# Pinned places for squares, scalings and weight sums, and later places for two parts of the first group's output norm, in a two-scheme gemm kernel

## The chip, the cores and the metric

The kernel runs on one core of one Trainium2 chip. The metric is the device time of one execution in microseconds (us); the median over the runs shown counts. TensorE (PE) does the matrix products, VectorE (DVE), ScalarE (ACT) and GpSimd (POOL) do the elementwise work, and SyncE (SP) and POOL hand transfers to the DMA queues.

## The reference, cut to what matters

One layer over 2048 prompt tokens and 8 sequences of 8 new tokens, all in fp32, at width 2048:

```python
z = rms_norm(x, pre_g)
xr, gr, u, v, gs = split(z @ w_in)            # five blocks of 1024 columns
xc, new_buf = causal_depthwise_conv(xr, conv_buf, conv_w, conv_b)
hr, h_last = rg_lru(xc, ...)                  # two gates per head, then a scan over the tokens
br = hr * silu(gr)
u = gelu(u); v = rms_norm(gelu(v), sgu_g)
bs = chunk_spatial_gating(u, v, w_s, b_s) * silu(gs)
out = concat([br, bs]) @ w_out
y = x + rms_norm(out, post_g)
```

The results are y for the prompt and for the samples, the convolution and scan states, and the samples' normed v.

## The kernel before, in words

**Precision.** Each fp32 product runs as three passes in fp32r: high times high, high times low, low times high. So each weight piece (128x1024) is loaded by SP into `wraw` (L179), its high part `wh` is made by ACT (L187) and its low part `wl` by DVE (L195), and PE waits for both.

**Group 0.** The tokens are cut into four groups of 512; the first also holds the 64 sample tokens, 576 columns in all. Its stage is a plain gemm (L370, and L381 for v) over jobs of two pieces each (some 6.4 us of PE a piece): the `xr` and `gr` jobs first, then `v`, then `gs` and `u`, then the 16 `out` jobs. After a pair of heads, `lru0` runs the recurrence: exp, tanh, square and square root on ACT, products and two scans on DVE (L484 to L505), one product on POOL (L485). The order of instructions on each engine in this stage is not the order in which the program hands them in: the tile scheduler sorts them by priority and by the readiness that its cost model expects. `later`, which is `tc.keep_in_program_order` (L95), pins an instruction behind the instruction of the same engine that was handed in just before it. That sets its place in the queue and nothing else; the data it waits for are as before.

**Sums for the other groups.** Groups 1 to 3 use a scheme with seven products in place of eight, which needs sums of weight quadrants. They are made beside group 0's gemm for 28 units: 16 units `c` (pairs of column blocks of the input weight; their sums run on DVE), four `w_v` and eight `w_or` (sums on POOL). A unit is four 512 KB quadrant loads (`load_quadrants`, L237, handed to POOL's DMA queue), four chained adds (`make_sums`, L248, L250, L252, L254) and four stores of the sums (L245, POOL's queue), named P_c, P_w_v and P_w_or. The program hands in unit n's loads at 45+20.5n us and its sums at 64+20.5n us of a plain estimate of PE's time (L1133 to L1137). The four quadrants lie in slots of a ring of 13 large buffers (`dbl`); slots are given out in the order in which the program hands the work in.

**Group 1's input.** During group 0's out jobs the squares of group 1's x are summed (`stat_load` L620, `stat_sum` L628, on ACT), the inverse roots are spread over the partitions (L637, L646), and the x rows are loaded and scaled (`z_raw`, `z_norm` L656, on DVE).

**Groups 1 to 3.** This part is a manual schedule: steps of one weight piece each, with lists of work that go ahead of a step's products (`tasks`) and behind them (`late`), issued in the order written. The loop hands in a step's `hi` work, its tasks, its `lo` work, its products and then its late list (L1332 to L1342).

**Group 0's output.** `norm_a "o"` and `norm_b "o"` (`row_rstd`, `row_bcast`) turn the sum of squares of group 0's output into a scale for each token: two products with a matrix of ones (nsAo, nsBo), DVE work, and two more products (nsCo, nsDo) whose input `dgo` DVE makes (L294, L300). They are on the late lists of steps 4 and 10 of group 1. `finish0_*` then does for each of 16 blocks: a load (L602), a DVE scaling (L606), an add of x by DMA (L609) and a store (L612). Blocks 0 to 7 begin at steps 12, 14, ... 26, and blocks 8 to 15 at V+3, V+5, ..., where V is step 56, the first of group 1's v products.

Of the kernel before, what the change touches and what calls it, by code (L numbers as in the profile page):

```python
# [11 lines left out]
AF = mybir.ActivationFunctionType  # L12
ALU = mybir.AluOpType
# [11 lines left out]
TP = 512  # L25
# [15 lines left out]
C_PRE, C_POST, C_CW, C_CB, C_BR, C_BI, C_LAM, C_SG = 0, 16, 32, 64, 72, 80, 88, 96  # L41
# [13 lines left out]
def hybrid_layer(ctx: ExitStack, tc: tile.TileContext, a):  # L55
    nc = tc.nc
# [35 lines left out]
    def col(base, i):  # L92
        return cv[:, base + i:base + i + 1]

    later = tc.keep_in_program_order  # L95
# [48 lines left out]
    state = {}  # L144
# [94 lines left out]
    def make_sums(unit):  # L239
        nm = "_".join(str(x) for x in unit)  # L240
        t = state.pop(("quad", unit))

        def put(k, x):
            sums[unit, k] = hp.tile([P, W], F32, name=f"{k}_{nm}")
            side.dma_start(sums[unit, k], x)  # L245

        eng = nc.vector if unit[0] == "c" else nc.gpsimd
        eng.tensor_add(t["B11"], t["B11"], t["B12"])  # L248
        put("P1", t["B11"])
        eng.tensor_add(t["B12"], t["B12"], t["B22"])  # L250
        put("P3", t["B12"])
        eng.tensor_add(t["B22"], t["B22"], t["B11"])  # L252
        put("P2", t["B22"])
        eng.tensor_add(t["B21"], t["B21"], t["B22"])  # L254
        put("P4", t["B21"])
# [367 lines left out]
    def stat_sum(g, n):  # L623
        c, b = divmod(n, 2)
        if n == 0:
            state["xss", g] = mp.tile([P, 4, 2], F32, tag="xss", name=f"xss{g}")
        x = state.pop(("xs", g, n))
        nc.scalar.activation(x, x, AF.Square, accum_out=state["xss", g][:, c, b:b + 1])  # L628

    def stat_rstd(g):  # L630
        sv = mp.tile([P, 4], F32, tag="xsv", name=f"xsv{g}")
# [21 lines left out]
    def z_norm(g, j, rows=(0, 1)):  # L653
        x = state["R", g, j]
        for i in rows:
            nc.vector.scalar_tensor_tensor(x[:, i, :TP], x[:, i, :TP], col(C_PRE, 2 * j + i), state["rB", g],  # L656
                                           op0=ALU.mult, op1=ALU.mult)

    def parts(key, j):
        lo, hi = state[(*key, j)], state.get((*key, 4 + j))  # L660
# [84 lines left out]
    early, tasks, late = defaultdict(list), defaultdict(list), defaultdict(list)  # L745

    def at2(s, f, *args):

        tasks[s].append((f, *args))
# [309 lines left out]
    for job in jobs:  # L1059
        kind, j = job  # L1060
# [9 lines left out]
    for s in steps:  # L1070
        for job, i in s:
            kind, j = job
# [41 lines left out]
    for hp_ in range(0, NH, 2):  # L1114
        i = jobs.index(("gr", NH + hp_ + 1))
# [18 lines left out]
    for n, u in enumerate(units):  # L1134
        for t, f in ((45 + 20.5 * n, load_quadrants), (64 + 20.5 * n, make_sums)):
            by_step[next(i for i, x in enumerate(when) if x >= t)].append((f, u))
    for n in range(8):  # L1137
        at(("out", 3 + n // 2), stat_load, 1, n)
        at(("out", 5 + n // 2), stat_sum, 1, n)
# [3 lines left out]
    for j in range(8):  # L1143
        at(("out", 8 + j // 2), z_raw, 1, j)
        at(("out", 11 + j // 3), z_norm, 1, j)
# [17 lines left out]
    for n, step in enumerate(steps):  # L1163
        for f, *args in by_step[n]:
            f(*args)
        job, i = step[0]
# [37 lines left out]
    for g in range(1, NG):  # L1204
        G = len(steps2)
        V, U, O, R2 = G + 56, G + 84, G + 140, G + 168
# [22 lines left out]
        wide(g, "v", "w_v", 0, put_v(g))  # L1229
        if g == 1:  # L1230
            for j in range(KT):
                t = 12 + 2 * j if j < 8 else V + 3 + 2 * (j - 8)
                at2(t, finish0_load, j)
                t += 3
                at2(t, finish0_scale, j)
                at2(t + 1, finish0_add, j)
                at2(t + 4, finish0_store, j)
        else:
            at2(G - 1, load_gq, g - 1, 1)
            for n in range(4):  # L1240
                k = (g - 1, (1, 1, 0, 0)[n], (3, 2, 2, 3)[n])
                t = G + (5, 7, 9, 11)[n]
                at2(t, finish_scale, *k)
                at2(t + 1, finish_add, *k)
                at2(t + 6, finish_store, *k)
            at2(V + 16, load_gq, g - 1, 0)
            for n in range(4):
                k = (g - 1, n % 2, n // 2)
                t = V + 21 + 3 * n
                at2(t - 5, finish_load, *k)  # L1250
                at2(t, finish_scale, *k)
                at2(t + 1, finish_add, *k)
                at2(t + 6, finish_store, *k)
# [31 lines left out]
        if g + 1 < NG:  # L1285
            for n in range(8):
                at2(O + 2 + 3 * n // 2, stat_load, g + 1, n)
                at2(O + 5 + 3 * n // 2, stat_sum, g + 1, n)
            at2(O + 17, stat_rstd, g + 1)
            late[O + 20].append((stat_spread, g + 1))  # L1290
            at2(O + 21, stat_take, g + 1)
            for j in range(8):
                at2(O + 18 + j, z_raw, g + 1, j)
                for i in range(2):
                    at2(O + 22 + 2 * j + i, z_norm, g + 1, j, (i,))
            key = ("R", g + 1)
            for j in range(4):
                combine(key, "A11", j, R2 + 2 + j)
                combine(key, "A22", j, R2 + 8 + j)
                at2(R2 + 10 + j, pre, key, "D3", j)  # L1300
                combine(key, "A12", j, R2 + 12 + j)
                at2(R2 + 14 + j, pre, key, "E", j)
                combine(key, "E", j, R2 + 16 + j)
                at2(R2 + 18 + j, pre, key, "D1", j)
                combine(key, "D1", j, R2 + 19 + j)
                combine(key, "D3", j, R2 + 23 + j)
                at2(R2 + 21 + j, pre, key, "F", j)
                combine(key, "F", j, R2 + 26 + j)
# [15 lines left out]
    at2(R2 + 28, last_rstd, 0)  # L1324
    for qq in range(4):
        at2(R2 + 29, last_both, 0, qq)
    late[4].append((norm_a, "o"))
    late[10].append((norm_b, "o"))

    base = pos_of[steps2[0][3]]  # L1330
    with tc.manual_schedule():
# [84 lines left out]
```

## Time and profile before

| | us |
|---|---|
| median of 3 runs (lowest, highest) | 2570.75 (2570.57, 2571.52) |
| profiled execution, own time | 2568.9 |
| profiled execution, span | 2567.1 |
| PE busy | 2497.7 (97% of the span) |
| DVE busy | 1748.8 (68%) |
| ACT busy | 1391.6 (54%) |
| POOL busy | 470.5 (18%) |
| mean granted TensorE clock | 0.991 of full speed |

The span goes from the first to the last instruction; 1.8 us of the execution's own time lie around it. Group 0 takes the first 797 us of the span, groups 1 to 3 the rest. A row of the timeline gives the start, the duration, the engine, the line, what is written from what, and in brackets how long the engine stood idle before it and what ended that. Busy shares are means over stages with different limits, so the rows below are cut by stage.

### The profile page before, as it was taken

How to read it: one execution, taken by the hardware profiler on the slowest of the kernel's cores; microseconds unless marked ns; L12 is line 12 of the kernel's file. 1: busy time of each engine (PE TensorE's matmuls, PEld its weight loads, DVE VectorE, ACT ScalarE, POOL GpSimd, SP SyncE). 2: the span in 40 equal slices, each digit the busy share in tenths (PEclk: the TensorE clock that was granted, in tenths of full speed). 3: DMA queues.
4: the chain of work that ended last, by engine and by line, in shares of the span. 5: the costliest groups of instructions: out<-in, count | busy, mean ns of one | idle time of the engine just before them, and what ended most of it. 6: DMA issues, size and time to landing. Idle time of an engine off the chain costs nothing.

```text
span 2567.1 us, 41558 instructions
## 1 busy us (share of the span) xinstructions
PE 2497.7 (97%) x16710; PEld 2300.2 (90%) x16710; DVE 1748.8 (68%) x2244; ACT 1391.6 (54%) x1777; POOL 470.5 (18%) x548
## 2 busy tenths in 40 slices
PE   7989999999999999999999999999999999999997
PEld 6989789999999998799878998799878998799886
DVE  7776155545466686756888686756888687756866
ACT  5444342223324577545756677545756577645654
POOL 4331024964751201100100100100000100100000
PEclk9999999999999999999999999999999999999999
DMA  6995389985964766756776755855776755855576
GB/s 226 332 328 214 107 286 322 369 276 193 323 221 155 228 210 207 233 182 187 268 260 197 239 192 180 252 178 186 258 274 197 240 177 185 254 192 181 187 253 198
DMA packets 167649, 587.11 MB, mean 229 GB/s; under 512 B 19216, under 2 KB 19776, under 8 KB 167456
## 3 DMA queue, kind: packets, MB, share of 16 engines
q1 hardware_dynamic: 107184, 378.11, 44.5%
q0 software_dynamic: 59696, 205.30, 24.0%
q8 instruction: 130, 2.13, 0.3%
q10 hardware_dynamic: 576, 1.05, 0.1%
q14 instruction: 63, 0.52, 0.1%
HBM read 494.92 MB, written 89.47 MB: 228 GB/s over the span
## 4 chain that ended last, share of the span: by engine, by line
PE 77%; DMA 7%; DVE 7%; ACT 5%; issue 3%; POOL 1%; SPq 0%; DVEq 0%; ACTq 0%; POOLq 0%
PE gm0out L370 8%; PE gm0v L381 4%; PE gm0gs L370 4%; PE gm0u L370 4%; PE gm0gr L370 3%; DMA wraw_c_P<-P_c 2%; PE gm0xr L370 2%; DVE wl_c_B L195 1%; DMA wraw_c_B<-w_in 1%; PE g L862 1%; PE sp L559 1%; PE w2o1a L716 1%; PE w2o1d L716 1%; PE w3o0d L716 1%; PE w1o1a L716 1%
## 5 line engine op out<-in xcount | busy, mean ns | idle before, releaser
L187 ACT ACTIVATE wh_c_P<-wraw_c_P 128x1024 fp32r<-128x1024 f32 x192 | 203.0, 1059 | 255.4 <-DMA wraw_c_P<-P_c 73.8
L195 DVE TENSOR_TENSOR wl_c_P<-wraw_c_P,wh_c_P 128x1024 fp32r<-128x1024 f32 x192 | 234.3, 1221 | 105.4 <-ACT wh_c_P L187 103.2
L195 DVE TENSOR_TENSOR wl_c_B<-wraw_c_B,wh_c_B 128x1024 fp32r<-128x1024 f32 x144 | 175.4, 1221 | 86.0 <-ACT wh_c_B L187 85.9
L187 ACT ACTIVATE wh_c_B<-wraw_c_B 128x1024 fp32r<-128x1024 f32 x144 | 152.2, 1058 | 147.6 <-DMA wraw_c_B<-w_in 24.8
L187 ACT ACTIVATE wh_w_or_P<-wraw_w_or_P 128x1024 fp32r<-128x1024 f32 x96 | 101.6, 1058 | 83.9 <-DMA wraw_w_or_P<-P_w_or 27.7
L195 DVE TENSOR_TENSOR wl_w_or_P<-wraw_w_or_P,wh_w_or_P 128x1024 fp32r<-128x1024 f32 x96 | 117.4, 1223 | 40.9 <-ACT wh_w_or_P L187 40.4
L187 ACT ACTIVATE wh_w_or_B<-wraw_w_or_B 128x1024 fp32r<-128x1024 f32 x72 | 76.1, 1059 | 79.6 <-DMA wraw_w_or_B<-w_or 15.8
L370 PE MATMUL gm0out<-c0l,wh_out 128*128 128x288 f32 x512 | 110.5, 297 | 1.0 <-DVE c0l L161 0.8
L370 PE MATMUL gm0out<-c0h,wh_out 128*128 128x288 f32 x512 | 110.7, 297 | 0.0
L370 PE MATMUL gm0out<-c0h,wl_out 128*128 128x288 f32 x512 | 110.1, 296 | 0.0
L195 DVE TENSOR_TENSOR wl_w_or_B<-wraw_w_or_B,wh_w_or_B 128x1024 fp32r<-128x1024 f32 x72 | 87.9, 1221 | 30.0 <-ACT wh_w_or_B L187 29.5
L195 DVE TENSOR_TENSOR wl_out<-wraw_out,wh_out 128x1024 fp32r<-128x1024 f32 x32 | 53.0, 1657 | 54.0 <-ACT wh_out L187 53.9
L620 POOL DMA_DIRECT2D xs<-xt x24 | 12.9, 538 | 391.5 <-PE sp L559 291.9
L370 PEld LDWEIGHTS gm0out<-c0l,wh_out 128*128 128x128 f32 x512 | 82.0, 188 | 1.6 <-DVE c0l L161 1.4
L431 POOL DMA_DIRECT2D wg<-w_g x16 | 11.9, 743 | 387.9 <-ACT xch L846 128.9
L370 PEld LDWEIGHTS gm0out<-c0h,wh_out 128*128 128x128 f32 x512 | 82.0, 188 | 0.6 <-issue 0.5
L370 PEld LDWEIGHTS gm0out<-c0h,wl_out 128*128 128x128 f32 x512 | 82.2, 188 | 0.0
L187 ACT ACTIVATE wh_out<-wraw_out 128x1024 fp32r<-128x1024 f32 x32 | 33.8, 1056 | 83.4 <-PE gm0out L370 51.6
L195 DVE TENSOR_TENSOR wl_w_v_P<-wraw_w_v_P,wh_w_v_P 128x1024 fp32r<-128x1024 f32 x48 | 58.5, 1221 | 29.6 <-ACT wh_w_v_P L187 29.6
L187 ACT ACTIVATE wh_w_v_P<-wraw_w_v_P 128x1024 fp32r<-128x1024 f32 x48 | 50.0, 1054 | 48.7 <-DMA wraw_w_v_P<-P_w_v 32.7
L370 PE MATMUL gm0gr<-z0h,wl_gr 128*128 128x288 f32 x256 | 57.3, 305 | 8.3 <-DVE wl_gr L195 8.3
L370 PE MATMUL gm0xr<-z0h,wh_xr 128*128 128x288 f32 x256 | 56.6, 303 | 7.2 <-ACT wh_xr L187 5.4
(1609 smaller groups left out, 8660.9 us busy)
## 6 DMA issues: line engine op xcount, KB each, us to landing
wraw_c_P<-P_c SPq DMA_DIRECT2D x192, 512.0 KB, 4.2
wraw_c_B<-w_in SPq DMA_DIRECT2D x144, 512.0 KB, 4.3
wraw_w_or_P<-P_w_or SPq DMA_DIRECT2D x96, 512.0 KB, 4.3
wraw_w_or_B<-w_or SPq DMA_DIRECT2D x72, 512.0 KB, 3.8
wraw_w_v_P<-P_w_v SPq DMA_DIRECT2D x48, 512.0 KB, 3.6
wraw_w_v_B<-w_v SPq DMA_DIRECT2D x36, 512.0 KB, 3.5
wraw_out<-w_out SPq DMA_DIRECT2D x32, 512.0 KB, 4.5
xs<-xt POOLq DMA_DIRECT2D x24, 512.0 KB, 5.8
```

Of the source, the lines that this page charges most:

```text
L187: nc.scalar.activation(h[:, sl], raw[:, sl], AF.Copy)
L195: nc.vector.tensor_sub(l[:, sl], raw[:, sl], h[:, sl].bitcast(F32))
L370: nc.tensor.matmul(p[:, :n], w, zz[:, o:o + n], start=(k == 0 and n_pass == 0), stop=(k == KT - 1 and n_pass == 2))
L381: nc.tensor.matmul(p[:n], zz[:, c * P:c * P + n], w, start=(k == 0 and n_pass == 0), stop=(k == KT - 1 and n_pass == 2))
L431: side.dma_start(w2.rearrange("p (h c) -> p h c", h=2), a["w_g"][hp_:hp_ + 2].rearrange("h p a c -> p h (a c)"))
L559: nc.tensor.matmul(p[:, c * P:(c + 1) * P], state["vn", c, h // 4][:, vs], wst[:, h, :], start=True, stop=True)
L620: side.dma_start(x, a[f"xt{g}"][c * P:(c + 1) * P, b * W:(b + 1) * W])
L716: nc.tensor.matmul(bks[b], zz, w, start=(not cont and kk == 0 and n_pass == 0), stop=(kk == HALF - 1 and n_pass == 2), skip_group_check=True)
L862: nc.tensor.matmul(p, ww[:, ws], xx[:, i, :TP], start=n_pass == 0, stop=n_pass == 2)
```

## The change: what it does

Three kinds of work of the first stage are pinned in the place at which the program hands them in: the first add of each `c` unit (the other three follow it through their data), the squares of group 1's x (`stat_sum` for g = 1), and the scaling of the first row of each x pair of group 1 (`z_norm`, row 0). For group 0's output, the two norm parts go from the late lists of steps 4 and 10 to those of steps 8 and 14, blocks 0 to 6 begin two steps later (14+2j), and block 7 moves from step 26 to V+1. Blocks 8 to 15 stay.

```diff
         eng = nc.vector if unit[0] == "c" else nc.gpsimd
-        eng.tensor_add(t["B11"], t["B11"], t["B12"])
+        i = eng.tensor_add(t["B11"], t["B11"], t["B12"])
+        if unit[0] == "c":
+            later(i)
...
-        nc.scalar.activation(x, x, AF.Square, accum_out=state["xss", g][:, c, b:b + 1])
+        i = nc.scalar.activation(x, x, AF.Square, accum_out=state["xss", g][:, c, b:b + 1])
+        if g == 1:
+            later(i)
...
-            nc.vector.scalar_tensor_tensor(x[:, i, :TP], x[:, i, :TP], col(C_PRE, 2 * j + i), state["rB", g],
-                                           op0=ALU.mult, op1=ALU.mult)
+            n = nc.vector.scalar_tensor_tensor(x[:, i, :TP], x[:, i, :TP], col(C_PRE, 2 * j + i), state["rB", g],
+                                               op0=ALU.mult, op1=ALU.mult)
+            if g == 1 and i == 0:
+                later(n)
...
-                t = 12 + 2 * j if j < 8 else V + 3 + 2 * (j - 8)
+                t = 14 + 2 * j if j < 7 else V + 1 + 2 * (j - 7)
...
-    late[4].append((norm_a, "o"))
-    late[10].append((norm_b, "o"))
+    late[8].append((norm_a, "o"))
+    late[14].append((norm_b, "o"))
```

## Rows read from the trace of the kernel before

**Rows 1.** The page's first part: busy time of each engine, share of the span, instructions.

```profile
PE 2497.7 (97%) x16710; PEld 2300.2 (90%) x16710; DVE 1748.8 (68%) x2244; ACT 1391.6 (54%) x1777; POOL 470.5 (18%) x548
```

**Rows 2.** The waits of PE over the whole span, grouped by what ran next and what ended the wait: us in total, times, longest us.

```profile
PE gm0gr L370 <- DVE wl_gr L195: 8.3, 2, 4.8
...
PE gm0out L370 <- DVE c0l L161: 0.8, 1, 0.8
```

**Rows 3.** Stretches of group 0's stage: length, then busy time (instructions) of PE, PEld, DVE, ACT and POOL, the granted clock, the DMA share and GB/s. 80 to 212 holds the xr and gr jobs, 212 to 312 the last of them and part of v, 420 to 557 gs and u.

```profile
80.00:212.00 132.00, 123.71 (x894) 121.67 (x893) 99.21 (x167) 64.02 (x87) 43.78 (x76) 0.97 0.93 336
212.00:312.00 100.00, 100.00 (x587) 87.44 (x586) 38.59 (x75) 36.76 (x46) 10.57 (x12) 1.00 0.37 126
...
420.00:557.00 137.00, 137.00 (x1025) 136.06 (x1024) 77.08 (x58) 35.53 (x37) 122.94 (x108) 1.00 0.96 343
```

**Rows 4.** The waits of DVE in the stretch 80 to 212 us: total, times, longest.

```profile
DVE pB11c L248 <- DMA pB12c<-w_in: 18.1, 5, 8.2
```

**Rows 5.** The timeline of DVE in group 0's xr and gr jobs, up to the second long stop of PE.

```profile
123.91 1.23 DVE L248 TENSOR_TENSOR pB11c<-pB11c,pB12c 128x1024 f32<-128x1024 f32 x1 [4.28 <-DMA pB12c<-w_in]
...
157.88 1.23 DVE L248 TENSOR_TENSOR pB11c<-pB11c,pB12c 128x1024 f32<-128x1024 f32 x1 [8.24 <-DMA pB12c<-w_in]
...
163.81 0.81 DVE L400 TENSOR_TENSOR xr<-gm0xr,rsBx 128x288 f32<-128x288 f32 x2
...
168.14 0.17 DVE L425 COPY ncs<-xsm 128x24 f32<-128x24 f32 x1
...
174.96 1.23 DVE L248 TENSOR_TENSOR pB11c<-pB11c,pB12c 128x1024 f32<-128x1024 f32 x1 [3.09 <-DMA pB12c<-w_in]
...
177.00 1.22 DVE L250 TENSOR_TENSOR pB12c<-pB12c,pB22c 128x1024 f32<-128x1024 f32 x1
...
180.32 1.22 DVE L195 TENSOR_TENSOR wl_gr<-wraw_gr,wh_gr 128x1024 fp32r<-128x1024 f32 x1
```

**Rows 6.** The timeline of ACT in the same stretch.

```profile
164.66 0.82 ACT L404 ACTIVATE xc<-xr,cv 128x512 f32<-128x512 f32 x1 [6.71 <-DVE xr L400]
...
173.53 1.99 ACT L187 ACTIVATE wh_gr<-wraw_gr 128x1024 fp32r<-128x1024 f32 x2
```

**Rows 7.** Short stretches around the second stop of PE (181 to 188) and around group 0's output norm (833 to 840), columns as in rows 3.

```profile
181.00:184.00 3.00, 2.41 (x10) 2.42 (x11) 3.00 (x9) 0.00 (x0) 1.07 (x2) 0.50 1.02 378
184.00:188.00 4.00, 4.00 (x21) 4.00 (x21) 4.00 (x12) 2.21 (x3) 2.11 (x4) 0.58 0.94 295
...
833.00:836.00 3.00, 2.06 (x3) 0.49 (x3) 0.84 (x2) 0.00 (x0) 0.00 (x0) 0.50 0.55 176
836.00:840.00 4.00, 4.00 (x21) 3.88 (x22) 1.96 (x3) 0.00 (x0) 0.00 (x0) 0.59 0.08 22
```

**Rows 8.** The timeline of PE around the output norm, first the one short wait ahead of it, then nsCo and nsDo, then the first products of three later steps.

```profile
827.57 0.39 PE L702 MATMUL q1xg0c<-R1D,wl_c_P 128*128 128x256 f32 x1 [0.48 <-DVE wl_c_P L195]
...
832.94 2.05 PE L296 MATMUL nsCo<-dgo,ones 128*128 128x512 f32 x2 [2.54 <-DVE dgo L294]
835.93 0.69 PE L302 MATMUL nsDo<-dgo,ones 64*128 64x64 f32 x2 [0.94 <-DVE dgo L300]
...
840.70 0.40 PE L702 MATMUL q1xg0d<-R1F,wh_c_B 128*128 128x256 f32 x2
...
846.35 0.40 PE L702 MATMUL q1xg1a<-R1A,wh_c_B 128*128 128x256 f32 x2
```

**Rows 9.** The timeline of DVE in the step from 846.35 us, and what follows it.

```profile
847.57 1.23 DVE L195 TENSOR_TENSOR wl_c_P<-wraw_c_P,wh_c_P 128x1024 fp32r<-128x1024 f32 x1 [0.27 <-ACT wh_c_P L187]
...
850.16 0.82 DVE L606 SCALAR_TENSOR_TENSOR fo<-fo,cv,rsBo 128x576 f32<-128x576 f32 x1
```

**Rows 10.** The timeline of POOL in group 1's v products: the load of a block of group 0's output, and the store behind it.

```profile
1018.02 0.55 POOL L602 DMA_DIRECT2D fo<-o  x1 [7.79 <-DVE t L887]
1018.66 0.55 POOL L612 DMA_DIRECT2D y<-fo  x1
```

**Rows 11.** The timeline of ACT in the same place.

```profile
1021.92 0.60 ACT L802 ACTIVATE vn<-w1va 128x512 f32<-128x512 f32 x1 [3.20 <-DMA y<-fo]
```

**Rows 12.** The timeline of POOL from gs and u up to the start of the out jobs.

```profile
437.86 2.38 POOL L250 TENSOR_TENSOR pB12w_v<-pB12w_v,pB22w_v 128x1024 f32<-128x1024 f32 x1
...
556.94 0.57 POOL L245 DMA_DIRECT2D P_w_or<-pB21w_or  x1 [0.30 <-POOL pB21w_or L254]
...
577.06 1.44 POOL L552 TENSOR_TENSOR u<-u,gs 128x576 f32<-128x576 f32 x1 [10.11 <-ACT u L551]
...
588.43 1.89 POOL L552 TENSOR_TENSOR u<-u,gs 128x576 f32<-128x576 f32 x1 [7.80 <-ACT u L551]
```

**Rows 13.** The timeline of DVE in gs and u: a low part of a weight, and the product behind which unit 15's first add is handed in.

```profile
438.30 3.02 DVE L195 TENSOR_TENSOR wl_u<-wraw_u,wh_u 128x1024 fp32r<-128x1024 f32 x1 [0.18 <-ACT wh_u L187]
...
442.29 2.10 DVE L582 TENSOR_TENSOR u<-u,s 128x576 f32<-128x576 f32 x1
```

**Rows 14.** The waits of ACT in group 0's out jobs (600 to 800 us): total, times, longest.

```profile
ACT xs L628 <- DMA xs<-xt: 27.4, 4, 9.5
```

**Rows 15.** The timeline of DVE at the norm of group 0's x: an add of unit 0, and the copy behind it.

```profile
64.16 1.23 DVE L250 TENSOR_TENSOR pB12c<-pB12c,pB22c 128x1024 f32<-128x1024 f32 x1
65.30 0.68 DVE L298 COPY rsBx<-nsCx 128x512 f32<-128x512 f32 x1
```

**Rows 16.** The timeline of POOL in the v jobs: a store of a sum that waits for its add.

```profile
314.42 0.54 POOL L245 DMA_DIRECT2D P_c<-pB11c  x1 [45.89 <-DVE pB11c L248]
```

## The prediction

> **What bounds the kernel now.** I read the page's busy times first: PE is busy for 97% of the span, the next engine for 68% [rows 1]. So the time is PE's work plus PE's stops, and a change that takes no product away can win no more than the stops and the products that ran at the lower clock. PE's waits come next [rows 2]: the costliest of those that this change can touch are two waits for `wl_gr`, the low part of a gr weight, 8.3 us together, the longer one 4.8. The table by stages shows where they lie: from 80 to 212 us the DMA share is 0.93 and DVE is busy for 99.2 of 132 us, while the next 100 us have 0.37 and 38.6 [rows 3]. DVE's waits in that stretch are the third view: 18.1 us in five waits, up to 8.2, all before the first add of a unit's sums, for its quadrant B12 [rows 4]. What stands behind such an add on DVE waits with it.
>
> The timeline shows both stops made that way [rows 5, 6]. An add waited 4.28 us until 123.91; that is the first, 3.5 us one (8.3 less 4.8). For the second, an add waited 8.24 us until 157.88; the copy of finished xr products (L400) came only at 163.81, behind it; ACT had waited 6.71 us for that copy at 164.66 and reached `wh_gr` at 173.53. Then another add waited 3.09 us until 174.96, a second add of the unit stood at 177.00, and `wl_gr` began at 180.32. When PE went on it ran at 1.2 instead of 2.4 GHz: granted clock 0.50 and 0.58 over 181 to 188 [rows 7]. Of 2.41 and 4.00 us of busy time, 2.41 x 0.50 + 4.00 x 0.42 = 2.9 us are lost to that.
>
> The other place is group 0's output norm: PE stood 0.48 us, 2.54 us before nsCo and 0.94 before nsDo [rows 8], and worked at clock 0.50 and 0.59 from 833 to 840: 2.06 x 0.50 + 4.00 x 0.41 = 2.7 us lost [rows 7].
>
> **Part a: the units' first adds.** No add, load or store is added; DVE's places change. The loads still start at the plain estimate, but a unit's first add now stands behind the DVE instruction handed in just before it. From the program's order I read that unit 2 stands behind a low part in xr's fifth job, unit 3 behind the state copies of the same job (the L425 of before, 168.14), units 4 to 6 at the end of the gr jobs, and units 7 to 11 in the v jobs, where DVE is busy for 38.6 of 100 us. In before all of units 0 to 9 were done by 212 us. So both adds that made the second stop leave it: unit 6's, with its 8.24 us, and unit 7's, whose 3.09 us of wait and two adds (1.23 + 1.22) ahead of `wl_gr` are 5.5 us against a stop of 4.8 [rows 5]. Unit 4's add, which made the first stop, goes behind gr's copies some 80 us later, when its quadrants have long landed. I take away 8.3 us of stops and 2.9 of clock: 11.2. Against it I put 1.5 us, an estimate from the 168.14 row: unit 3's four adds of 1.23 now stand in the recurrence's work (4.9 us), where the removed adds leave a cushion of 5.5 less 4.8 plus what the 8.24 leaves. Value -9.7, bounds -11.2 and 0 (the stops come back elsewhere).
>
> The moved adds drag stores and loads along in POOL's queue: each unit's four stores wait there, and the next loads and POOL's products stand behind them. Before, a store waited 45.89 us in the v jobs and PE did not stop for it [rows 16]; that cover is the v jobs' light load.
>
> **Part b: norm parts at steps 8 and 14.** In before DVE was behind when it came to `dgo`: PE had nothing else to run. At step 14 DVE has finished its low part at 847.57 + 1.23 = 848.8; `dgo` (0.68, estimate from equal tiles, as the 0.82 scale is the next larger) would end near 849.5. PE's step from 846.35 ends at 846.35 + 2.83 = 849.2 (2.83: half of the two steps from 840.70 to 846.35) [rows 8, 9]. So about 0.1 to 0.3 us of the 2.54 stays, 0.94 stays before nsDo, and stops that short I expect to leave the clock at 2.4 GHz: it was at 1.2 only once the stop of 2.54 had passed [rows 7, 8]. Gain: 0.48 + 2.44 + 2.7 = 5.6. What is late next: the norm's DVE work now sits in steps 14 to 16, ahead of the taps and low parts of steps 16 and 17; the 0.82 us scale at 850.16 [rows 9] leaves that place, and two diagonals and two copies (some 2.5 us with their waits, an estimate) come. I take +1.0. Value -4.6; bounds -5.6 and +1 (the stop merely moves, and the low parts come late).
>
> **Part c: block 7 among the v products.** All sixteen blocks pass the same ring. One more load, add and store in the v part: POOL waited 7.79 us for a slot there, the store behind it at 1018.66 made ACT wait 3.20 [rows 10, 11]. By my reading of the slots block 9's load comes later by up to 8 us, but the scalings have about 2 us of room. Value +0.5, bounds -1 (one block less among the quads) and +4.4 (one more wait of 3.20 and its sequel of 1.2).
>
> **Part d: the tail of the sums.** Unit 15 now stands behind the product at 442.29 [rows 13] instead of before 420. The w_v and w_or sums behind it on POOL need its slots, so POOL's chain, which held 122.9 of 137 us and ended at 556.94 [rows 3, 12], ends some 19 us later, near 576. POOL then stood idle 10.11 and 7.80 us before its products at 577.06 and 588.43 [rows 12], which cover most of it, and the loads behind them set the 0.8 us stop at the start of the out jobs [rows 2]. Value +1.0, bounds 0 and +5 (two adds of 2.4 in front of a product).
>
> The Trainium skill has a rule that speaks against this part ("SBUF — State Buffer", "SBUF: two separate sides"): a VectorE instruction with two SBUF inputs and a GpSimd instruction that reads SBUF lock each other out for the whole instruction. The trace agrees: a `wl_u` took 3.02 us beside a POOL add of 2.38 [rows 12, 13], where others take 1.22 [rows 5]. What that would make of unit 15 is among the rivals.
>
> **Part e: small ones.** Unit 0's add at 64.16 stood before the copy of group 0's x norm at 65.30 [rows 15]; it goes away from there: -0.3 (0 to -0.5). The squares of group 1's x cost nothing: ACT waited 27.4 us for their transfers without a stop of PE [rows 14], and pinned they come later, so these waits shrink. The scaling of group 1's x ends near 782 by my count of DVE's out-job work, 15 us before PE's first product of group 1 at 797. Without that cover every late microsecond would be one of PE; I put 0.
>
> **The sum.** -9.7 - 4.6 + 0.5 + 1.0 - 0.3 = -13.1 on the profiled execution: 2568.9 - 13.1 = 2555.8. The median stands 1.85 above the profiled execution (2570.75), so 2557.7.
>
> **The rivals.**
> 1. The second stop stays: the recurrence's own work on ACT, 8.9 us from 164.66 to 173.53 [rows 6], and unit 3's adds set `wl_gr`, not unit 6's wait. Against it: the 8.24 and 3.09 us waits sit right in the chain. Price 4.8 + 2.9 = 7.7 given back: 2565.3.
> 2. Part b gains nothing, since DVE is behind at step 14 too: +4.6, 2562.3. For it: DVE has a step's work in every step; against: `dgo`'s place 0.3 us after the step's end.
> 3. The tail of the sums runs into the out jobs: part d at +5, 2561.7.
> 4. DVE and POOL get in each other's way behind 442.29. `wl_u` took 3.02 us beside an add of POOL that took 2.38 [rows 12, 13]; if unit 15's four adds each waited as long, they would hold DVE for 4 x (2.4 + 1.23) = 14.5 us. A piece takes PE 6.4 us and low parts are made ahead by nearly two pieces, so I count 11.5 us of it as covered and 3 us as a stop: 2560.6. Against it: POOL's chain waits for unit 15's slots.
> 5. Slower: POOL's queue becomes the place where things stop. A store of a sum, pinned late, blocks POOL's product of the recurrence (L485) behind it; 45.89 us of such a wait were seen [rows 16]. If that happens in two recurrences of the gr jobs, PE stands for the wait of an add, 8.2 us [rows 4], twice, and part a is lost: -13.1 + 9.7 + 16.4 = +13, 2583.7. It decides once the product is more than one piece (6.4 us of PE) late. Against: the recurrences that lie among pinned adds are those whose units have landed long before.
> 6. The pin does not bite, as the instruction before it floats too: parts a, d and e fall away, about 2566.6.
>
> **How the numbers follow.** Forecast 0.43; rivals 0.20, 0.12, 0.08, 0.03, 0.10 and 0.04 in that order. This kernel's measurement tells 0.2% (5.1 us) from no change: faster is below 2565.6, slower above 2575.9. Rival 1 lies on the border and goes half to "same"; so do rival 6 and a third of rivals 2 and 3, for the cases in which two of them meet. Faster: 0.42 + 0.10 + 0.08 + 0.05 + 0.03 = 0.68; slower 0.10; same 0.22. The range goes from the lower bounds together (-11.2 - 5.6 - 1 - 0.5 = -18.3, 2552.4, and a little for clock elsewhere: 2551) to rivals 1 and 6 with some spread: 2569. The likeliest case alone is 2552 to 2562.
>
> **What would show it.** Part a: no wait of DVE for B12 in 80 to 212 us, no stop of PE before `wl_gr`, clock 1.00 there; DMA share under 0.93 in 80 to 212 and over 0.37 in 212 to 312. Part b: nsCo three steps or more later, its stop under 0.5 us, no clock of 0.5 around it. Part c: the wait for y's store beside the v products. Part d: the last P_w_or store near 576, the stop before `c0l`. Wrong would be: stops before `wl_gr` or `wh_gr` in the gr jobs of a new cause, POOL's product L485 late behind P_c stores, or stops behind nsDo for low parts.

## The result, and the profile after

The changed kernel takes 2558.36 us (median of 7 runs, 2551.35 to 2562.32) beside 2570.64 for the kernel before (7 runs, 2564.45 to 2575.18). The ratio is 0.9941, 95% interval 0.992 to 0.9962; the forecast was 2557.7 in a range of 2551 to 2569. One kernel's runs differ by some 10 us, so the parts are read from the stages of the profiles, and the times only carry the sums. The profiled execution of the changed kernel took 2551.54, span 2549.6, near the shortest of its runs. A few runs of some kernels, with a mean clock of 0.85 or less over the whole run, took 2690 us and more and are left out of every time below.

The page's first part: the same number of instructions on every engine, and 6.5 us less of PE's busy time than in [rows 1].

```profile
PE 2491.2 (98%) x16710; PEld 2294.5 (90%) x16710; DVE 1758.6 (69%) x2244; ACT 1391.6 (55%) x1777; POOL 469.1 (18%) x548
```

The waits of PE over the whole span (us in total, times, longest). A wait of PE is called a stop below. The row of `wl_gr` that led [rows 2] is gone, and nsCo waits 0.4 instead of 2.54 [rows 8].

```profile
...
PE gm0out L372 <- DVE c0l L161: 1.0, 2, 0.8
...
PE q1xg1d L708 <- DVE wl_c_B L195: 1.0, 1, 1.0
...
PE nsDo L304 <- DVE dgo L302: 0.9, 1, 0.9
...
PE nsCo L298 <- DVE dgo L296: 0.4, 1, 0.4
```

The stretches of [rows 3], same columns. PE is busy throughout both (123.71 of 132 before) at full clock; the DMA share has moved from the first stretch (0.93 before) to the second (0.37 before).

```profile
80.00:212.00 132.00, 132.00 (x979) 130.44 (x978) 91.62 (x161) 68.25 (x92) 33.09 (x51) 1.00 0.66 232
212.00:312.00 100.00, 100.00 (x554) 85.04 (x554) 55.58 (x86) 40.62 (x58) 25.21 (x44) 1.00 0.74 270
```

DVE in the gr jobs, the place of [rows 5]: the first add of unit 3 stands right behind the copy of the states, as handed in. It waits for nothing, and `wl_gr` follows it at once. In 80 to 212 us no wait of DVE is for a quadrant any more (18.1 us in [rows 4]); the largest row of DVE's waits there is shown first, then the timeline.

```profile
DVE wl_xr L195 <- ACT wh_xr L187: 12.5, 5, 5.2
```

```profile
176.66 1.22 DVE L195 TENSOR_TENSOR wl_gr<-wraw_gr,wh_gr 128x1024 fp32r<-128x1024 f32 x1
...
180.37 0.17 DVE L427 COPY ncs<-xsm 128x24 f32<-128x24 f32 x1
180.45 1.22 DVE L248 TENSOR_TENSOR pB11c<-pB11c,pB12c 128x1024 f32<-128x1024 f32 x1
181.59 1.22 DVE L195 TENSOR_TENSOR wl_gr<-wraw_gr,wh_gr 128x1024 fp32r<-128x1024 f32 x1
```

Group 0's output norm, on PE and then on DVE. The two products take 1.10 us (2.05 in [rows 8]); `dgo` comes right behind a low part that ends at 830.38.

```profile
831.12 1.10 PE L298 MATMUL nsCo<-dgo,ones 128*128 128x512 f32 x2 [0.37 <-DVE dgo L296]
833.16 0.43 PE L304 MATMUL nsDo<-dgo,ones 64*128 64x64 f32 x2 [0.94 <-DVE dgo L302]
```

```profile
829.15 1.23 DVE L195 TENSOR_TENSOR wl_c_P<-wraw_c_P,wh_c_P 128x1024 fp32r<-128x1024 f32 x1 [0.41 <-ACT wh_c_P L187]
830.29 0.68 DVE L296 TENSOR_TENSOR dgo<-ident,rsTo 128x512 f32<-128x512 f32 x1
```

POOL at the end of the sums, the place of [rows 12]: the last store of a w_or sum is handed over at 563.18, and the first loads for the out jobs stand right behind it. PE's first out product is at 577.9 (588.1 before). So POOL is through 14.1 us ahead of it, where the kernel before had 30.6. This time, from the end of the last such store to PE's first out product, is called the lead below, and the late end of the sums is called the tail. In the kernel before the loads `cb` did not stand right behind the last store: they began at 564.81, 23.3 us ahead of PE.

```profile
563.18 0.57 POOL L245 DMA_DIRECT2D P_w_or<-pB21w_or  x1 [0.30 <-POOL pB21w_or L256]
563.75 2.14 POOL L345 DMA_DIRECT2D cb<-cat  x4
566.88 1.42 POOL L554 TENSOR_TENSOR u<-u,gs 128x576 f32<-128x576 f32 x1 [0.99 <-ACT u L553]
```

The same loads in the kernel before:

```profile
564.81 2.14 POOL L343 DMA_DIRECT2D cb<-cat  x4
```

The stages of every profile, in us, each from the first product of one kind to that of the next: xr and gr from nsCx to v; out from the first out product to group 1; xg from there to group 1's v products; v to the u products; last, groups 2 and 3 to the end of the span. Not in the table are the time up to nsCx (63.0 to 64.9), group 0's v, gs and u products (329.4 in all but the two kernels with three pins: 329.6 in three_units_pinned, 331.7 in three_pins_and_norm) and group 1's u and out products (322.4 to 324.8).

| kernel | xr, gr | out | xg | v | groups 2, 3 |
|---|---|---|---|---|---|
| before | 195.7 | 208.9 | 180.6 | 89.9 | 1176.5 |
| changed | 184.6 | 209.4 | 173.8 | 92.5 | 1171.8 |
| changed_again | 184.5 | 209.3 | 174.4 | 93.2 | 1175.6 |
| only_unit_pins | 184.7 | 212.3 | 181.9 | 90.3 | 1180.0 |
| without_unit_pins | 193.0 | 209.0 | 175.2 | 91.8 | 1176.5 |
| only_norm_late | 194.9 | 208.9 | 176.6 | 90.0 | 1174.1 |
| only_blocks_late | 192.9 | 209.2 | 180.3 | 91.7 | 1174.2 |
| three_units_pinned | 184.6 | 209.0 | 184.3 | 90.2 | 1174.2 |
| block7_at_28 | 184.2 | 212.0 | 176.3 | 91.7 | 1176.6 |
| units_0_to_11_pinned | 183.7 | 208.9 | 174.7 | 92.2 | 1181.0 |
| both_mended | 184.6 | 209.1 | 175.4 | 90.3 | 1172.3 |
| both_mended_again | 184.7 | 208.9 | 175.5 | 89.0 | 1178.6 |
| without_x_pins | 184.3 | 212.1 | 173.7 | 91.7 | 1179.2 |
| three_pins_and_norm | 184.4 | 208.8 | 175.8 | 90.5 | 1184.9 |

### The profile page after: what moved, and what is told of

It reads as the page before. It is cut to its first block, busy times and chain, and to the rows that moved or that the text cites. A ratio compares the mean times of both kernels' runs of the same rounds, so it can differ in the third digit from the quotient of the medians.

```text
span 2549.6 us, 41563 instructions
## 1 busy us (share of the span) xinstructions
PE 2491.2 (98%) x16710; PEld 2294.5 (90%) x16710; DVE 1758.6 (69%) x2244; ACT 1391.6 (55%) x1777; POOL 469.1 (18%) x548
## 4 chain that ended last, share of the span: by engine, by line
PE 78%; DMA 7%; DVE 6%; ACT 6%; issue 3%; POOL 0%; SPq 0%; DVEq 0%; ACTq 0%
PE gm0out L372 8%; PE gm0v L383 4%; PE gm0gr L372 4%; PE gm0gs L372 4%; PE gm0u L372 4%; PE gm0xr L372 3%; DMA wraw_c_B<-w_in 1%; PE g L868 1%; DMA wraw_w_v_P<-P_w_v 1%; DMA wraw_w_or_P<-P_w_or 1%; PE sp L561 1%; DVE wl_c_B L195 1%; DMA wraw_c_P<-P_c 1%; PE w2o1a L722 1%; PE w3o0d L722 1%
## 5 line engine op out<-in xcount | busy, mean ns | idle before, releaser
L195 DVE TENSOR_TENSOR wl_w_or_P<-wraw_w_or_P,wh_w_or_P 128x1024 fp32r<-128x1024 f32 x96 | 117.4, 1223 | 44.3 <-ACT wh_w_or_P L187 43.9
L383 PE MATMUL gm0v<-wh_v,z0l 128*128 128x512 f32 (+1 forms) x160 | 63.2, 396 | 0.0
```

Of the source, the lines that this page charges most:

```text
L195: nc.vector.tensor_sub(l[:, sl], raw[:, sl], h[:, sl].bitcast(F32))
L383: nc.tensor.matmul(p[:n], zz[:, c * P:c * P + n], w, start=(k == 0 and n_pass == 0), stop=(k == KT - 1 and n_pass == 2))
```

## The experiments

**Each part alone, and the whole without its first part.** The unit pins in the kernel before:

```diff
-        eng.tensor_add(t["B11"], t["B11"], t["B12"])
+        i = eng.tensor_add(t["B11"], t["B11"], t["B12"])
+        if unit[0] == "c":
+            later(i)
```

> Part a alone in the kernel before. My theory (a unit's add that waits for its quadrant holds up what stands behind it on DVE): no stop of PE before wl_gr, no wait of DVE for B12 in 80 to 212 us, PE's first product of group 1 (797.0 before) at 787 to 788, the stops of 0.48, 2.54 and 0.94 us at the output norm as before; time 9.7 us under the kernel before. Rival (the stops come back elsewhere in group 0): first product of group 1 at 793 or later, time within 4 us of before.

The stage came out as expected: 184.7 us, no stop for `wl_gr`. The time did not: group 1 began at 791.2, and the ratio to the kernel before is 0.9988 (0.9975 to 1.0), some 3 us saved, at the edge of none, where 9.7 were expected. Of the 11.0 us that this profile gained in the stage, the out jobs gave 3.4 back (212.3 us against 208.9); 1.3 more went in xg, where the stop before q1xg1d grew from 2.01 to 3.18 us with clock 0.57 over 883 to 887, and 3.5 in groups 2 and 3, which the change does not touch. The rows of the out jobs show how; first POOL, where the loads `cb` stand behind the last store, 13.1 us ahead of PE's first out product at 578.9 (the lead).

```profile
565.22 0.57 POOL L245 DMA_DIRECT2D P_w_or<-pB21w_or  x1 [0.30 <-POOL pB21w_or L256]
565.79 2.14 POOL L345 DMA_DIRECT2D cb<-cat  x4
```

Then DVE: four low parts of the late `cb` stand ahead of the copy of the finished u products, which comes at 580.45 (577.08 in the changed kernel's profile).

```profile
577.78 2.76 DVE L161 TENSOR_TENSOR c0l<-cb,c0h 128x576 fp32r<-128x576 f32 x4
580.45 0.81 DVE L402 TENSOR_TENSOR u<-gm0u,rsBx 128x288 f32<-128x288 f32 x2
581.19 1.21 DVE L195 TENSOR_TENSOR wl_out<-wraw_out,wh_out 128x1024 fp32r<-128x1024 f32 x1
582.32 0.74 DVE L567 SCALAR_TENSOR_TENSOR s<-sp,cv,bsb 128x512 f32<-128x512 f32 x1
```

And PE, which stops before a spatial product for the accumulator that DVE still has to read:

```profile
583.12 1.16 PE L561 MATMUL sp<-wst,vn 128*128 128x128 f32 x8 [2.06 <-DVE s L567]
```

Next, the changed kernel without these pins:

```diff
-        if unit[0] == "c":
-            later(i)
...
```

> The changed kernel with the first adds of the units left to the scheduler. My theory: both stops before wl_gr are back (3.5 and 4.8 us, clock at half behind the longer one), group 1 begins within 2 us of 797.0, the output norm is as in the changed kernel; time about 3.4 us under the kernel before (-4.6 + 0.5 + about 0.7). Rival (the pins of the squares or scalings carry part of the gain): group 1 begins at 793 or earlier.

The stops are back, here 4.76 us with clock 0.50 behind it (136 to 139 us) and 2.20 without, and the jobs take 193.0 us; DVE waits for B12 again. Group 1 began at 794.8, a little over 2 us from 797.0. The ratio is 0.9981 (0.9971 to 0.9991), -4.9 us against the -3.4 expected. The pins of the squares and scalings carry none of that stage's gain. The stops on PE, and DVE's waits in 80 to 212 us:

```profile
135.66 0.84 PE L370 MATMUL gm0gr<-z0h,wl_gr 128*128 128x288 f32 x2 [4.76 <-DVE wl_gr L195]
...
181.87 0.53 PE L370 MATMUL gm0gr<-z0h,wl_gr 128*128 128x288 f32 x2 [2.20 <-DVE wl_gr L195]
```

```profile
DVE pB11c L248 <- DMA pB12c<-w_in: 17.6, 6, 7.4
```

The norm parts alone:

```diff
-    late[4].append((norm_a, "o"))
-    late[10].append((norm_b, "o"))
+    late[8].append((norm_a, "o"))
+    late[14].append((norm_b, "o"))
```

> Part b alone: the two norm parts on the late lists of steps 8 and 14, blocks of the output where they were. My theory: the stop before nsCo under 0.5 us instead of 2.54, that before nsDo 0.9 as before, no clock at half around them; from the first product of group 1 to the first v product 4.6 us less than before (180.6 us there), 5.6 at most; time 4.6 us under. Rival (DVE is behind at step 14 too): nsCo still waits 2 us or more and the stretch is within 1 us of before.

nsCo waited 0.75, a little more than expected, nsDo 0.94, and the clock stayed at full around them. It fell later: the stop before q1xg1d grew from 2.01 (row below, kernel before, clock 1.00) to 2.88 us, and the clock was 0.50 from 884 to 887. The xg stretch fell from 180.6 to 176.6 us all the same; the ratio is 0.9986 (0.9973 to 1.0), -3.6. The rival is out.

```profile
841.14 1.10 PE L296 MATMUL nsCo<-dgo,ones 128*128 128x512 f32 x2 [0.75 <-DVE dgo L294]
843.17 0.43 PE L302 MATMUL nsDo<-dgo,ones 64*128 64x64 f32 x2 [0.94 <-DVE dgo L300]
```

```profile
PE q1xg1d L702 <- DVE wl_c_B L195: 2.0, 1, 2.0
```

The places of the blocks alone:

```diff
-                t = 12 + 2 * j if j < 8 else V + 3 + 2 * (j - 8)
+                t = 14 + 2 * j if j < 7 else V + 1 + 2 * (j - 7)
```

> Part c alone: blocks 0 to 6 of group 0's output two steps later, block 7 at V+1. My estimate of +0.5 stands against the upper bound of +4.4: by the first the stretch from the first v product of group 1 to the first u product stays within 1 us of before (89.9 us); by the second it grows by 2 us or more through waits of PE for wh and wl of w_v, as it did in the changed kernel (92.5 us). Time +0.5 against +2 to +4.

The v stretch grew by 1.8 us, between the two. The ratio is 1.0016 (1.0006 to 1.0025), +4.1 us; its profile, taken in the shortest of its runs, shows 1.5 of it (xg and v together 272.0 against 270.5); where the rest lies is not settled.

**The blocks and the tail, one by one and together.** Both edits are made in the changed kernel. First blocks 0 to 7 all two steps later than in the kernel before, and blocks 8 to 15 as there; then the pins on units 0 to 11 only:

```diff
-                t = 14 + 2 * j if j < 7 else V + 1 + 2 * (j - 7)
+                t = 14 + 2 * j if j < 8 else V + 3 + 2 * (j - 8)
```

> The changed kernel with block 7 of group 0's output at step 28 (14+2j up to j = 7) and blocks 8 to 15 at V+3 to V+17, as before. If block 7 at V+1 costs the v products: the stretch from the first v product to the first u product comes back from 92.5 to 90 us and the time is about 2 us under the changed kernel's (2558.4 beside 2570.6 for the kernel before, so 14 under the kernel before). If the stretch grew for another reason (the shorter products before it, or a passing clock): it stays at 91.5 us or more and the time is the changed kernel's.

Ratio 0.9959 (0.9945 to 0.9973). The expectation missed in two places. The v stretch came down only to 91.7 in this profile; in the three others that have block 7 at step 28 it is 89.0 to 90.5. And the out jobs took 212.0 us, with a stop of 2.40 us before the spatial product, as in the kernel with the unit pins alone, and with 13.0 us of lead: the tail. The xg stretch took 176.3, where it had 173.8 with block 7 elsewhere. One block less among the quads and one more among the v products nearly cancel.

```diff
-        if unit[0] == "c":
+        if unit in units[:12]:
             later(i)
```

> The changed kernel with the first adds pinned for units 0 to 11 alone; units 12 to 15 are left to the scheduler as before. My theory on the tail: the last store of a w_or sum ahead of the out jobs comes 25 us or more before PE's first out product (30.6 us in the kernel before, 14.1 in the changed one), the out jobs take 208.9 us, and the xr and gr jobs stay at 184.6; time 0 to 3 us under the changed kernel's. Rival (the slots of the later units are late anyway, because the earlier units hold them): the tail stays within 3 us of the changed kernel's and nothing changes.

The rival fell: the last store comes 30.2 us ahead of PE's first out product (576.5), the out jobs take 208.9 us, and the xr and gr jobs keep their gain. The ratio 0.9951 (0.9934 to 0.9968) does not tell it from the changed kernel.

```profile
545.70 0.57 POOL L245 DMA_DIRECT2D P_w_or<-pB21w_or  x1 [0.57 <-POOL pB21w_or L256]
552.47 0.55 POOL L587 DMA_DIRECT2D cat<-u  x1 [6.20 <-DVE u L584]
553.01 2.15 POOL L345 DMA_DIRECT2D cb<-cat  x4
```

> Both of the last two together: units 0 to 11 pinned, block 7 at step 28. By the sum of my two theories the time is 2 to 5 us under the changed kernel's, 14 to 17 under the kernel before, with 184.6 us for the xr and gr jobs, 208.9 for the out jobs and 90 for the v products. By the rivals it is the changed kernel's time within 1 us.

All three stages as expected; ratio 0.9942 (0.9923 to 0.9961), 2553.77 us. These runs alone cannot tell it from the changed kernel, so both were measured again, side by side, in the last group of runs below.

**Three pins: order or load.** In the kernel before:

```diff
+        if unit in [units[n] for n in (4, 6, 7)]:
+            later(i)
```

> The kernel before with the pin on the first adds of units 4, 6 and 7 alone, those whose waits stood ahead of the two stops. My theory (DVE's order, not the load of the transfers, made the stops): both stops before wl_gr are gone or under 1 us and the xr and gr jobs take 186 us or less, although the loads of units 0 to 3 and 5 still come early and the DMA share in 80 to 212 us stays above 0.75. Rival (the transfers' load delayed the weights, and the pins helped by thinning it out): with that load the stops stay, 2 us or more each, and the jobs take 190 us or more.

Three pins give the whole stage: 184.6 us, no stop before `wl_gr`, and of DVE's waits for quadrants 0.6 us are left. Ratio 0.9972 (0.9956 to 0.9988). The share of the transfers stands at 0.74 in 80 to 212 us, just under the 0.75 that I had named, since the pinned units also delay loads behind them. So the load was lower than before here too, and a kernel with the load at 0.93 and DVE's order mended was not run. The rival's own path, late weights, is ruled out by the trace of the kernel before: the weight whose high part ACT made at 173.53 had been handed in at 147.83 and had landed at 155.7, and that of the first stop had landed at 103.0, where ACT made its high part at 126.43. The four weights handed in from 141.9 to 165.8 us all landed within 9.3 us:

```profile
L179 SPq DMA_DIRECT2D wraw_gr<-w_in x4: 327/328/328, 141.9 to 165.8; - x4
DMA to landing us min/median/max: 3.8/7.6/9.3
```

What came late were the quadrants, and through them DVE. Whether the stops would be gone at a lower load alone, with DVE's order as before, is open. The gain of the stage did not all reach the end here either: in xg the stop before q1xg1d was 4.09 us with clock 0.50 behind it, and xg took 184.3 us. DVE's wait for a quadrant and the stretch:

```profile
DVE pB21c L256 <- DMA pB21c<-w_in: 0.6, 1, 0.6
```

```profile
80.00:212.00 132.00, 132.00 (x979) 130.44 (x978) 89.37 (x163) 69.27 (x93) 37.01 (x58) 1.00 0.74 269
```

**The last group, on one chip.**

> The changed kernel once more, beside the next three on one chip. If the tail of the sums stands at the edge of its cover, its out jobs take anything from 209 to 212.5 us in a profile, with or without a stop before the spatial product, and the v products take 91.5 to 92.5. Time 11 to 15 us under the kernel before.

2553.68 us beside 2567.84, ratio 0.9938 (0.9922 to 0.9954). Out jobs 209.3, lead 14.8 us, no stop before the spatial product. The v stretch at 93.2 us is above the 91.5 to 92.5 expected; the mean clock in it was 0.96, against 0.98 in the first profile.

> Units 0 to 11 pinned and block 7 at step 28, once more, beside the changed kernel. My theory: 209 us for the out jobs in this profile too and about 90.3 for the v products; 2 to 5 us under the changed kernel beside it. Rival (both are within what one run differs from the next): no difference that its interval tells from none.

2555.78 us, ratio 0.9944 (0.993 to 0.9959): the rival holds, the two kernels cannot be told apart. In its profile the out jobs are 0.4 us shorter, xg 1.1 longer and v 4.2 shorter, and groups 2 and 3, where the two kernels are alike, take 3.0 more. PE's largest waits in the v products, of the changed kernel's second profile and then of this one:

```profile
PE w1vb L722 <- ACT wh_w_v_P L187: 2.4, 2, 1.8
PE w1vb L722 <- DVE wl_w_v_P L195: 2.3, 2, 1.7
PE w1vd L722 <- DVE wl_w_v_B L195: 0.8, 1, 0.8
PE w1vc L722 <- DVE wl_w_v_P L195: 0.6, 1, 0.6
```

```profile
PE w1vd L722 <- DVE wl_w_v_P L195: 2.2, 2, 1.7
PE w1vb L722 <- ACT wh_w_v_P L187: 1.5, 1, 1.5
PE w1vb L722 <- DVE wl_w_v_P L195: 0.8, 1, 0.8
```

Both still have the wait for `wh` that follows from the store of a block, as in [rows 11]; in the changed kernel's second profile ACT waits 3.20 us for it again.

```profile
1008.63 0.60 ACT L808 ACTIVATE vn<-w1va 128x512 f32<-128x512 f32 x1 [3.20 <-DMA y<-fo]
```

The changed kernel without the pins of the squares and the scaling:

```diff
-        if g == 1:
-            later(i)
...
-            if g == 1 and i == 0:
-                later(n)
```

> The changed kernel without the pins of the squares and of the scaling of group 1's x. My forecast put these at nothing: the out jobs and all stages as in the changed kernel, time within 1.5 us of it. Rival (they keep the start of the out jobs or of group 1 free): a stop before the spatial product or at the first products of group 1 of 1 us or more in this profile alone, and a time 2 us or more above the changed kernel's.

2557.1 us (median of 8 runs), ratio 0.9958 (0.9942 to 0.9973), 3.4 us above the changed kernel in its median with intervals that overlap. Its profile has a stop of 1.87 us before the spatial product and 212.1 us of out jobs, with 13.5 us of lead. That looks like the rival, but the kernel with block 7 at step 28 has both x pins and the same stop. So the tail is enough to explain it, and nothing shows a gain or a loss of these pins.

The parts that had shown a gain, with block 7 at step 28, and nothing else; the edit is against the kernel before:

```diff
+        if unit in [units[n] for n in (4, 6, 7)]:
+            later(i)
...
-                t = 12 + 2 * j if j < 8 else V + 3 + 2 * (j - 8)
+                t = 14 + 2 * j if j < 8 else V + 3 + 2 * (j - 8)
...
-    late[4].append((norm_a, "o"))
-    late[10].append((norm_b, "o"))
+    late[8].append((norm_a, "o"))
+    late[14].append((norm_b, "o"))
```

> Pins on units 4, 6 and 7 alone, the two norm parts at steps 8 and 14, all of blocks 0 to 7 at 14+2j, no other pin. By the sum of the parts that showed a gain, with neither the late tail nor block 7 at V+1: 184.6 us for the xr and gr jobs, 209 for the out jobs, 175 to 176 from the first product of group 1 to its first v product, 90.3 for the v products; time 0 to 5 us under the changed kernel's, as both mended ends. Rival (the norm part gains only with the scaling pinned, or all units have to be pinned together): 3 us or more above the changed kernel's.

2553.55 us, ratio 0.9948 (0.993 to 0.9967), with the four stages as expected. But a new stop stands just behind the first of them, in the v jobs: PE waited 2.06 us at 256.5 for the copy of finished gr products.

```profile
PE gm0v L383 <- DVE gr L402: 2.1, 1, 2.1
```

On DVE that copy stood at 256.01, behind adds of three units (their first adds at 237.43, 244.29 and 252.36) and low parts, with no idle time between. In three_units_pinned the same order had the copy at 253.73 and no such stop; in the changed kernel it is at 253.56. So the kernel with three pins stands at an edge of its own there. In time this version is level with the changed kernel, and no version that was run beats the changed kernel by more than the measurement can tell.

## Why the prediction was right, and where its terms were off

**Part a (-9.7).** Right in mechanism and size. The changed kernel's stage is 11.1 us shorter than in the profile on which the sum rests, and about 9.5 shorter than the mean of the four profiles without unit pins (194.1). The 1.5 us that I held back for unit 3's adds was wrong as an account: they stand where I said, and PE did not stop. That the adds of units 4, 6 and 7 made the two stops is shown by the kernel with three pins, and rival 1 is out with it; which of them made which stop was read from the rows and not tried one by one. In time the part alone showed less: by ratio 3.1 us with all units pinned and 7.2 with three; the whole (15.2) less the whole without it (4.9, in another group of runs) is some 10.

**Part b (-4.6).** Right. Alone it gave 4.0 us of the xg stretch in its profile and 3.6 (0 to 6.9) in time. The rest of 0.1 to 0.3 us that I expected before nsCo was 0.37 in the changed kernel and 0.75 alone, nsDo's 0.94 stayed to the digit, and the lower clock did not come there. The late low parts that I charged with 1.0 us did not show as a stop in the steps right behind nsDo. A price of that kind came some 40 us later, with the part alone: 0.9 us more before q1xg1d and the clock at half behind it. In the changed kernel that stop is 0.96, and 1.31 in its second profile, with the clock at full; why was not tried. Rival 2 is out.

**Part c (+0.5).** Right by the stages of the later kernels, through two terms that I had only as bounds; not right by the time of the part alone, which was 4.1 us (1.5 to 6.4) longer. With the norm late, xg and v together take 266.5 us with block 7 at V+1 (mean of the changed kernel twice, units_0_to_11_pinned and without_x_pins) and 266.1 with it at step 28 (mean of block7_at_28, both_mended twice and three_pins_and_norm): 2.0 us more among the v products, 1.6 less among the quads. The mean clock in these v stretches was 0.98, 0.96, 0.96 and 1.00 with block 7 at V+1 and 0.98, 0.98, 1.00 and 0.98 with it at step 28, so, as an estimate from these figures, nearly half of the 2.0 us is clock, which differs between two profiles of the changed kernel. What only the six profiles with block 7 at V+1 have, and all of them, is one more stop before a w1vb product for `wl_w_v_P`, of 0.99 to 1.69 us, some 44 us into the stretch. In four of the six ACT also has a second wait for y's store in the v stretch, of 4.17 to 4.84 us (4.77 at 994.09 in the changed kernel); so the wait that I priced at 3.20 and 1.2 for the upper bound did come, and PE paid less for it.

**Part d (+1.0).** The place was right, the size too small. The last store at 576 on the old time line would have left 12 us to the first out product, and 13.0 to 14.8 were measured. But I read POOL's idle time as cover. What counts is how far ahead of PE the loads for the out jobs stand: 23.3 us before, when they waited for their data and not for the last store, and in the changed kernel the whole lead of 14.1. That is the edge: with 13.0 to 13.5 us of lead three profiles lost some 3 us (212.0 to 212.3), with 14.1 and 14.8 two lost 0.4 to 0.5. The mean of the five is 2.1 us. It is rival 3 at 3.1 to 3.4 of its 5 us where it comes, and it comes in some runs and not in others: block7_at_28, which lost 3.1, has the same group 0 as the changed kernel.

**Part e (-0.3), and the squares and scalings at 0.** The first gr product comes at 43.6 us before and at 43.9 to 45.6 in the other profiles, whether unit 0 is pinned or not, so the start itself hides 0.3 us. PE's wait at the copy shows it: 0.77 us in all eight profiles with unit 0 pinned, 0.98 to 1.08 in the six without. So part e gave 0.2 us. The row before and after:

```profile
PE gm0gr L370 <- DVE xr L400: 1.0, 1, 1.0
...
PE gm0gr L372 <- DVE xr L402: 0.8, 1, 0.8
```

The last scaling of group 1's x begins at 762.5 in the changed kernel and PE needs its results at 787.3: the cover I counted on was there.

**The other rivals.** Rival 4: unit 15's adds stand where I put them, behind the product of the first spatial head, and ran in 1.21 to 1.23 us each, since POOL had no add to run meanwhile (it handed over transfers and waited up to 2.06 us for its loads); the `wl_u` behind them took 3.41 us beside POOL's next add, and PE did not stop. Rival 5: no stop of PE goes back to POOL's product of the recurrence. Rival 6 is out by the row at 180.45.

**The sum.** -13.1 was forecast. By ratio it is 15.2 us (9.8 to 20.6), by medians 12.3. The two profiled executions differ by 17.4, of which 4.7 lie in groups 2 and 3, where the change touches nothing: in that comparison this much is luck.

The times of the parts do not add up to that of the whole. By ratio the unit pins alone saved 3.1 us, the norm parts alone 3.6, and the places of the blocks alone cost 4.1: 2.6 saved in sum, against 15.2 and, in the second measurement of the changed kernel, 15.9. The stages show some of what the parts do for each other: with the pins and the norm at its old place, the stop before q1xg1d was 3.18 us and, with three pins, 4.09, with the clock at half behind it, and neither is seen in the changed kernel. The rest is not settled, and my sum of independent terms had no place for it.

## What to carry to other kernels

Here chains of adds that waited for transfers held up all that stood behind them on their engine. So look in the waits of the engine, not of the bottleneck, for the first instruction whose data come late, and move just those: here three of sixteen pins took away both stops. When such work is moved back, measure how far ahead of the bottleneck the next hand-over stands, since here idle time on the engine that did the work was no cover. Where runs differ by more than a part is worth, compare the parts by stages between two landmarks of the same profile.

## What the runs showed that I had not expected

Groups 2 and 3 run the same order of instructions in all these kernels, and yet take 1171.8 to 1184.9 us from one profile to the next (two profiles of the changed kernel: 1171.8 and 1175.6). Their stops come and go at the same few products, as the waits of PE show: the changed kernel first, then three_pins_and_norm.

```profile
PE q3ug0a L708 <- DVE wl_c_B L195: 2.5, 1, 2.5
PE q2ug0a L708 <- DVE wl_c_B L195: 1.6, 2, 1.1
```

```profile
PE q2ug0a L704 <- DVE wl_c_B L195: 3.6, 2, 3.2
PE q3ug0a L704 <- DVE wl_c_B L195: 3.6, 2, 3.2
```

What decides between the two outcomes was not tried.

By the times, an instruction of DVE was held up here by more than one of POOL. Of 16 low parts of gs in the changed kernel (minimum, median and longest in ns) one took 7.65 us from 469.42 on, six times the usual, while POOL ran an add of a w_v sum (2.41 us from 468.64), a product (1.43 from 471.58) and another add (2.41 from 473.56), with only transfers handed over between them; the longest of the kernel before took 5.36. The Trainium skill's rule that I weighed under part d ("SBUF — State Buffer", "SBUF: two separate sides") has the loser blocked for the other's instruction; here the low part's time spans three of POOL's. That the shared access is the cause was not tried. PE stopped for neither.

```profile
L195 DVE TENSOR_TENSOR wl_gs<-wraw_gs,wh_gs x16: 1206/1228/7647, 350.4 to 529.9; 128x1024 fp32r<-128x1024 f32 x16
```

The length of a stop alone does not tell whether the lower clock follows. In the kernel before, the stop of 2.54 us before nsCo was followed by it [rows 7] and the longer one of 3.5 us before `wl_gr`, at 134 us, was not (granted clock 1.00 from 131 to 142).
